# Channel order of the normalised activations, 2 KB pieces of the first expert table, and a buffer of its own for row gathers

## The chip, the cores and the metric

The kernel runs on one NeuronCore of one Trainium2 chip. The metric is the device time of one execution in microseconds (us); the median of 3 runs is what two kernels are compared by. TensorE (PE) multiplies, VectorE (DVE) and ScalarE (ACT) do elementwise work, GpSimd (POOL) issues the gathers by index here, SyncE (SP) and ACT issue the other transfers (DMA), which all share 16 DMA engines.

## The reference, cut to what matters

One layer of a decoder, for 256 prompt tokens and 32 sample tokens (288 columns in all), D = 2048 channels, float32: attention and convolution, the output projection `w_out`, then the expert layer PEER with 16384 experts, then a gate, then the final norm. PEER is the part that the change touches:

```
xc   = rmsnorm(h, ffn_norm)
qh   = xc @ peer_wq                        # product keys pick 8 x 16 experts a token
eidx, g = top-16 of the key sums, softmax
hpre = einsum('cd,ced->ce', xc, u[eidx])   # u, v: 16384 x 2048 each (128 MB each)
act  = gelu(hpre) * g
h   += einsum('ce,ced->cd', act, v[eidx])
```

## The kernel before

Activations lie transposed: `hT[p, dt, token]` holds channel on 128 partitions and 16 blocks `dt`. Every float32 product is made of three matmuls of a high and a low part (`tri`, lines 200 to 202), so each weight tile is split by ACT (`h`, line 186) and DVE (`l`, line 187) into two.

For the 256 prompt tokens the kernel does not gather: it multiplies by all 16384 experts in 128 tiles `t` of 128 experts. A **u tile** is loaded (`u_load`, `ur`, 1 MB in 8 DMAs of 32 partitions, four on SP and four on ACT), transposed in 32x32 blocks by DVE (`uT`, L923), split, and multiplied (`up`, 48 matmuls); GELU gives `ac`. The weights g are written out as a dense table in DRAM (`Gd`, `Gl`) by a one-hot stage and read back as `gt`. The **v loop** goes over 32 groups `g` of 4 tiles and 4 column blocks `u`, so 128 v steps: a 1 MB block of `peer_v` is loaded (`v`, L216, one DMA of 128 partitions on SP), split, multiplied by four `ac` tiles (`vps`, 48 matmuls in four PSUM banks) and added to `hT` by DVE (L490). 25 u tiles are made ahead, the other 103 inside the loop.

The 32 sample tokens do use gathers: 64 times POOL fetches 128 picked rows (1 MB, `fetch`, L1116): first 32 rows of `peer_u` (`ug`), each reduced with `xr` on DVE (L1135), then 32 rows of `peer_v` (`vg`), each added to `acc` on DVE (L1145). One `next(picked)` of `between` is one gather; the line of the loop says at which steps.

`raw_tile` gives the 1 MB buffers into which weights and gathered rows land: one ring of three (`WR`), handed out in program order to v blocks, `w_in`, `w_out`, `peer_wq` and `ple_gate` blocks, and to gathers alike. The order of instructions on each engine comes from a scheduler that simulates the program when it is built; engines take their own instructions strictly in that order, and so do the queues of SP, ACT and POOL.

Ahead of PEER, `w_out` streams (`wa0` to `wa3`) end in `residual`: DVE adds to `hT`, ACT squares (`sqh`, L485), DVE sums (`sq`). From the sum come `n2r` and the broadcast `rb2` (buffer `rb`); then `xf`, the normalised activations, is made block by block and `peer_wq` (`pq0` to `pq6`) is multiplied.

Of the kernel before, what the change touches and what calls it, by code (L numbers as in the profile page):

```python
# [10 lines left out]
F32 = mybir.dt.float32  # L11
# [124 lines left out]
def body(ctx: ExitStack, tc: tile.TileContext, A, O):  # L136
# [27 lines left out]

    conv_b, ln_g, ln_b = (cvec[:, 8 * i:8 * i + 8] for i in range(3))

    def raw_tile(name):
        return wp.tile([P, D], F32, tag="wr", name=name, bufs=WR)

    marks = {}  # L170

# [29 lines left out]
        nc.tensor.matmul(ps, ah, bl, start=False, stop=False)  # L201
        nc.tensor.matmul(ps, al, bh, start=False, stop=last)  # L202

    def load_block(src, b, cols, rows_by_lane, name, after=(), by_lane=False):
        n = sum(c[1] for c in cols)
        raw = raw_tile(name)
        v = raw[:, :4 * n].rearrange("p (j c) -> p j c", j=4)
        rows = src[512 * b:512 * b + 512]
        at = 0
        for c0, m in cols:  # L210
            if rows_by_lane:
                for a in range(4):
                    nc.sync.dma_start(v[32 * a:32 * a + 32, :, at:at + m],
                                      rows[128 * a:128 * a + 128, c0:c0 + m].rearrange("(j r) c -> r j c", j=4))
            else:
                nc.sync.dma_start(v[:, :, at:at + m], rows[:, c0:c0 + m].rearrange("(j p) c -> p j c", j=4))  # L216
            at += m
        with ExitStack() as order:
            for i in after:
                order.enter_context(tc.issue_after(i.ins))  # L220
            h, l = split(wp, raw[:, :4 * n], D, "w8", name, WB, by_lane)
        if by_lane:
            return lambda k, j, q=4 // cut[0]: [x[:, 512 * q * (k // q) + P * (q * j + k % q):][:, :P] for x in (h, l)]
        return lambda k, j, w=P: [x.rearrange("p (j c) -> p j c", j=4)[:, k, P * j:P * j + w] for x in (h, l)]
# [72 lines left out]
    def wide_pair(name):  # L297
        return [wide.tile([P, ND, T], F32R, tag="wide", name=f"{name}{k}") for k in "hl"]
# [494 lines left out]
    for k in range(CT):  # L793
        part(cat[:, k], xc[0][:, k], xc[1][:, k])
    sq2 = pa.tile([P, T], F32, tag="rb", name="sq2")
    for u in range(4):
        for j, ps in enumerate(stream(A["w_out"][0], [(512 * u, 512)], 4, xc, False, f"wa{u}", (0, 1), by_lane=True)):
            residual(pa, 4 * u + j, ps[:, :T], sq2, "sqh")
    ps_rb2 = spread(rstd_cols(pa, [sq2], D, "n2"), "ps_rb2")
    rb2 = keep.tile([P, T], F32, tag="rb2", name="rb2")  # L800
    marks["rb2"] = nc.vector.tensor_copy(rb2, ps_rb2[:, :T])
    pa_stack.close()

    cut[0] = 2
# [11 lines left out]
    pick = ab.tile([P, 3, TP], F32, tag="pick", name="pick")  # L816
    tk_stack = ExitStack()
    tk = tk_stack.enter_context(tc.tile_pool(name="tk", bufs=1, reuse_waits=RW))

    xf = wide_pair("xf")  # L820
    for dt in range(ND):
        f = tk.tile([P, T], F32, tag="nf", name=f"xf_{dt}", bufs=2)
        nc.vector.scalar_tensor_tensor(f, hT[:, dt], gain(1, dt), rb2, op0=ALU.mult, op1=ALU.mult)
        part(f, xf[0][:, dt], xf[1][:, dt])

    iob = tk.tile([P, 16, 16], BF16, tag="iob", name="iob")
    nc.gpsimd.tensor_copy(iob, iota[:, :16, None].to_broadcast([P, 16, 16]))
# [78 lines left out]
    def u_load(t):  # L906
        if t >= NE or t in urs:
            return
        ur = ff.tile([P, D], F32, tag="u8", name=f"ur{t}", bufs=UB)
        for k in range(2):  # L910
            rows = A["peer_u"][0, P * t + 64 * k:P * t + 64 * k + 64].rearrange("(c b) (u a x) -> a c b u x", c=32, a=4, x=P)
            for a in range(4):
                getattr(nc, UQ[a]).dma_start(
                    ur[32 * a:32 * a + 32, 1024 * k:1024 * k + 1024].rearrange("c (b u x) -> c b u x", b=2, u=4), rows[a])
        urs[t] = ur

    def u_steps(t):
        u_load(t)
        u_load(t + 1)
        ur = urs.pop(t)  # L920
        uT = ff.tile([P, D], F32, tag="u8", name=f"uT{t}", bufs=UB)
        for k in range(2):
            nc.vector.transpose(uT.rearrange("p (u j k c b) -> p k b u j c", u=4, j=4, k=2, c=32)[:, k],  # L923
                                ur.rearrange("p (k b u j r) -> p k b u j r", k=2, b=2, u=4, j=4)[:, k])
        hr, lr = split(ff, uT, D, "u8", f"u{t}", UB)
        mm = None
        for u in range(5):
            if u > 0:
                mm = mm or mm_ps(f"up{t}")
                for dt in range(4 * u - 4, 4 * u):  # L930
                    s = slice(P * dt, P * dt + P)
                    tri(mm[:, :TP], (hr[:, s], lr[:, s]), (xf[0][:, dt, :TP], xf[1][:, dt, :TP]), dt == 0, dt == ND - 1)
            if u < 4:
                yield
        ac = ff.tile([P, T], F32, tag="ac", name=f"ac{t}", bufs=AB)[:, :TP]
        nc.scalar.activation(ac, mm[:, :TP], AF.Gelu)  # L936
        if t < LS:
            nc.sync.dma_start(Ad[t], ac)
        else:
            acts[t] = ac  # L940
        yield
# [13 lines left out]
    PQA = [marks[k] for k in PQK]  # L955
    for h in range(NH):
        if h % 2 == 0:
            qps = stream(A["peer_wq"][0], [(256 * h, 512)], 4, xf, True, f"pq{h}",
                         after=lambda b: PQA if h == 0 and b >= PQN else ())
        skT = sub_keys(h)  # L960
        qh = tk.tile([P, 2, T], F32, tag="qh", name=f"qh{h}", bufs=1)
        for n in range(2):
            nc.scalar.copy(qh[:, n], qps[2 * (h % 2) + n][:, :T])
        if h % 4 == 0:
            pss = ax_ps(f"pss{h}")
        for n in range(2):
            nc.tensor.matmul(pss[32 * (h % 4):32 * (h % 4) + 32, P * n:P * n + P], qh[:, n, TP:T], skT[:, n],
                             start=True, stop=True, tile_position=(0, 32 * (h % 4)))
        psp = ax_ps(f"psp{h}")
        for i in range(2):  # L970
            for n in range(2):
                c0 = 256 * i + 128 * n
                nc.tensor.matmul(psp[:, c0:c0 + P], qh[:, n, 128 * i:128 * i + 128], skT[:, n], start=True, stop=True)
        for i in range(2):
            for n in range(2):
                c0 = 256 * i + 128 * n
                sixteen(val[:, 2 * h + i, n], ind[:, 2 * h + i, n], psp[:, c0:c0 + P], P, f"wk{h}{i}{n}")
        if h >= 6:
# [76 lines left out]
    def v_part(g, between):  # L1055
# [11 lines left out]
            nc.vector.tensor_mul(v, v, gts[t // GK][:, :, t % GK])  # L1067
            hl.append(split(gpool, acts[t], TP, "ah", f"a{t}", AHB))
        for u in range(4):
            at = load_block(A["peer_v"][0], g, [(512 * u, 512)], False, f"v{g}_{u}", by_lane=True)  # L1070
            for j in range(4):
                ps = ax_ps(f"vps{g}_{u}{j}")
                for k in range(GRP):
                    tri(ps[:, :TP], at(k, j), hl[k], k == 0, k == GRP - 1)
                residual(None, 4 * u + j, ps[:, :TP], None, "")
            between(u)
            if last:
                gated_norm(range(4 * u, 4 * u + 4))
# [33 lines left out]
                nc.vector.tensor_add(sq3, sq3, q)  # L1112

    def fetch(src, s, name):
        gb = raw_tile(name)
        nc.gpsimd.indirect_dma_start(out=gb, out_offset=None, in_=src,  # L1116
                                     in_offset=bass.IndirectOffsetOnAxis(ap=eix[:, s // 16, s % 16:s % 16 + 1], axis=0))
        return gb

    def picked_steps():  # L1120
        xs = raw_tile("xs")
        c = slice(TP, T)
        x4 = [x[:, :, c].bitcast(F32)[:, :, None, :].to_broadcast([P, ND, 4, TS]) for x in xf]
        nc.vector.tensor_tensor(out=xs.rearrange("p (d a t) -> p d a t", d=ND, a=4), in0=x4[0], in1=x4[1], op=ALU.add)
# [1 line left out]
        for u in range(4):  # L1126
            ps = ax_ps(f"xsp{u}")
            for j in range(4):
                dt = 4 * u + j
                nc.tensor.transpose(ps[:, P * j:P * j + P], xs[:, P * dt:P * dt + P], ident)  # L1130
            nc.scalar.copy(lanes(xr[:, 512 * u:512 * u + 512]), turn(ps))
        gb = fetch(A["peer_u"][0], 0, "ug0")
        yield
        for s in range(32):
# [7 lines left out]
        for s in range(32):  # L1142
# [27 lines left out]
    for g in range(NE // GRP):  # L1170
        reload(g + 1)
        if g == NE // GRP - SIDE:
            gB = side_inputs()
        if g == NE // GRP - 1:
            xg = wide_pair("xg")
            sq3 = ff.tile([P, T], F32, tag="ac", name="sq3", bufs=AB)
        v_part(g, lambda u: (u_next(GRP * g + GRP + LK), next(picked, None) if g < 4 or u % 2 else None))
    gp_stack.close()
    pc_stack = ExitStack()
    pc = pc_stack.enter_context(tc.tile_pool(name="pc", bufs=1, reuse_waits=RW))  # L1180
# [78 lines left out]
```

## Time and profile before

| what | value |
|---|---|
| median of 3 runs (lowest, highest) | 2391.47 us (2390.91, 2402.99) |
| the profiled execution | 2391.9 us |
| its span, first to last instruction | 2389.9 us |
| granted TensorE clock, mean | 0.975 of full |
| PE, DVE, ACT busy | 94%, 81%, 42% of the span |
| bytes moved by DMA | 479.29 MB, 201 GB/s |

In the rows below, an "x" is a count of instructions, and a wait is idle time of an engine put down to what ended it. Numbers of windows are microseconds from the start of the span.

### The profile page before, as it was taken

How to read it: one execution, taken by the hardware profiler on the slowest of the kernel's cores; microseconds unless marked ns; L12 is line 12 of the kernel's file. 1: busy time of each engine (PE TensorE's matmuls, PEld its weight loads, DVE VectorE, ACT ScalarE, POOL GpSimd, SP SyncE). 2: the span in 40 equal slices, each digit the busy share in tenths (PEclk: the TensorE clock that was granted, in tenths of full speed). 3: DMA queues.
4: the chain of work that ended last, by engine and by line, in shares of the span. 5: the costliest groups of instructions: out<-in, count | busy, mean ns of one | idle time of the engine just before them, and what ended most of it. 6: DMA issues, size and time to landing. Idle time of an engine off the chain costs nothing.

```text
span 2389.9 us, 44695 instructions
## 1 busy us (share of the span) xinstructions
PE 2250.0 (94%) x17715; PEld 2205.2 (92%) x17715; DVE 1933.2 (81%) x3343; ACT 1007.0 (42%) x1623; POOL 165.2 (7%) x168
## 2 busy tenths in 40 slices
PE   6999999889889898999999999999999999999997
PEld 5999989889789888999999999999999999999997
DVE  5999844699989788989888787878888887877854
ACT  3453344343478533344333333333434343334533
POOL 2033140000000011100000000000000000000000
PEclk9999999999989998999999999999999999999998
DMA  7757442784558999999788798888989888975663
GB/s 197 172 125 172 107 142 89 168 170 87 132 146 217 260 282 279 300 260 269 245 233 238 212 241 224 222 237 219 243 222 241 213 230 221 237 211 172 169 134 83
DMA packets 474175, 479.29 MB, mean 201 GB/s; under 512 B 35785, under 2 KB 361825, under 8 KB 465374
## 3 DMA queue, kind: packets, MB, share of 16 engines
q1 hardware_dynamic: 306894, 309.03, 49.6%
q10 hardware_dynamic: 154672, 93.74, 16.5%
q0 software_dynamic: 12400, 73.66, 9.4%
q8 instruction: 139, 2.28, 0.4%
q14 instruction: 70, 0.57, 0.1%
HBM read 454.17 MB, written 23.00 MB: 200 GB/s over the span
## 4 chain that ended last, share of the span: by engine, by line
PE 49%; DMA 24%; DVE 13%; issue 10%; ACT 2%; SPq 1%; ACTq 0%; POOL 0%; DVEq 0%; POOLq 0%
DMA ur<-in_peer_u 7%; DMA vg<-in_peer_v,eix 7%; DMA v<-in_peer_v 5%; PE vps L200 4%; PE vps L202 4%; PE vps L201 4%; PE up L201 3%; PE up L202 3%; PE up L200 3%; DVE uT L923 3%; DMA gt<-Gd 1%; DVE v_0l L187 1%; DMA Gd<-stg 1%; DVE hT L490 1%; DMA gt<-Gl 1%
## 5 line engine op out<-in xcount | busy, mean ns | idle before, releaser
L923 DVE STREAM_TRANSPOSE uT<-ur 128x1024 f32<-128x1024 f32 x256 | 304.0, 1221 | 24.5 <-PE up L201 11.1
L490 DVE TENSOR_TENSOR hT<-hT,vps 128x256 f32<-128x256 f32 x512 | 199.4, 410 | 20.4 <-PE vps L202 20.2
L936 ACT ACTIVATE ac<-up 128x256 f32<-128x256 f32 x128 | 49.3, 387 | 369.1 <-DVE hT L490 114.7
L1145 DVE SCALAR_TENSOR_TENSOR acc<-vg,hot,acc 128x2048 f32<-128x2048 f32 x31 | 72.9, 2352 | 120.0 <-DMA vg<-in_peer_v,eix 120.0
L1135 DVE CUSTOM_DVE_ANT_0 ug<-ug,xr 128x2048 f32<-128x2048 f32 x32 | 73.1, 2286 | 29.0 <-DMA ug<-in_peer_u,eix 28.9
L1116 POOL DMA_INDIRECT ug<-in_peer_u,eix x32 | 39.6, 1238 | 749.6 <-DVE uT L923 324.6
L186 ACT CAST v_0h<-v 128x1024 fp32r<-128x1024 f32 x64 | 63.8, 1044 | 58.5 <-PE vps L201 32.0
L186 ACT CAST v_3h<-v 128x1024 fp32r<-128x1024 f32 x64 | 63.8, 1046 | 42.6 <-PE vps L201 20.7
L1116 POOL DMA_INDIRECT vg<-in_peer_v,eix x32 | 30.0, 937 | 746.4 <-DVE v_3l L187 367.8
L187 DVE TENSOR_TENSOR v_0l<-v,v_0h 128x1024 fp32r<-128x1024 f32 x64 | 75.7, 1216 | 6.1 <-ACT v_0h L186 6.1
L186 ACT CAST v_2h<-v 128x1024 fp32r<-128x1024 f32 x64 | 63.8, 1045 | 39.5 <-PE vps L201 24.0
L187 DVE TENSOR_TENSOR v_1l<-v,v_1h 128x1024 fp32r<-128x1024 f32 x64 | 75.7, 1215 | 2.4 <-ACT v_1h L186 2.4
L1041 PE MATMUL gp<-at,bt 128*128 128x128 f32 x512 | 68.0, 280 | 9.5 <-ACT at L1034 6.0
L187 DVE TENSOR_TENSOR v_2l<-v,v_2h 128x1024 fp32r<-128x1024 f32 x64 | 75.7, 1215 | 1.1 <-ACT v_2h L186 1.1
L187 DVE TENSOR_TENSOR v_3l<-v,v_3h 128x1024 fp32r<-128x1024 f32 x64 | 75.7, 1212 | 0.9 <-ACT v_3h L186 0.9
L1041 PEld LDWEIGHTS gp<-at,bt 128*128 128x128 f32 x512 | 62.9, 194 | 11.7 <-ACT at L1034 7.4
L186 ACT CAST v_1h<-v 128x1024 fp32r<-128x1024 f32 x64 | 64.0, 1046 | 19.1 <-DMA v<-in_peer_v 12.6
L1034 ACT ACTIVATE at<-eqa,pick 128x128 f32<-128x128 bf16 x192 | 64.3, 428 | 4.2 <-DVE eqa L1031 2.7
L457 DVE SCALAR_TENSOR_TENSOR cat<-cat,cw 128x256 f32<-128x256 f32 x120 | 52.7, 479 | 0.0
L1067 DVE TENSOR_TENSOR ac<-ac,gt 128x256 f32<-128x256 f32 x112 | 43.4, 391 | 8.0 <-DMA gt<-Gl 4.9
L1044 ACT COPY stg<-gp 128x256 f32<-128x256 f32 x128 | 41.8, 395 | 16.7 <-PE gp L1041 6.2
L1038 DVE TENSOR_TENSOR bt<-iota,pick 128x512 f32<-128x512 f32 x64 | 43.2, 679 | 0.0
(5771 smaller groups left out, 9874.7 us busy)
## 6 DMA issues: line engine op xcount, KB each, us to landing
v<-in_peer_v SPq DMA_DIRECT2D x128, 1024.0 KB
ur<-in_peer_u SPq DMA_DIRECT2D x512, 128.0 KB
ur<-in_peer_u ACTq DMA_DIRECT2D x512, 128.0 KB
Gd<-stg SPq DMA_DIRECT2D x14, 1024.0 KB
gt<-Gd ACTq DMA_DIRECT2D x32, 448.0 KB
gl0b<-in_w_in SPq DMA_DIRECT2D x32, 128.0 KB
gl1b<-in_w_in SPq DMA_DIRECT2D x32, 128.0 KB
gl2b<-in_w_in SPq DMA_DIRECT2D x32, 128.0 KB
```

What stands on the lines that cost most here:

```text
L186: marks["part"] = nc.scalar.copy(y, x)
L187: marks["sub"] = nc.vector.tensor_sub(z, x, y.bitcast(F32))
L200: nc.tensor.matmul(ps, ah, bh, start=first, stop=False)
L201: nc.tensor.matmul(ps, ah, bl, start=False, stop=False)
L202: nc.tensor.matmul(ps, al, bh, start=False, stop=last)
L490: nc.vector.tensor_add(x, x, ps)
L923: nc.vector.transpose(uT.rearrange("p (u j k c b) -> p k b u j c", u=4, j=4, k=2, c=32)[:, k], ur.rearrange("p (k b u j r) -> p k b u j r" ...
L1034: nc.scalar.activation(at[:, k], eq[:, :, k], AF.Copy, scale=pick[:, 2, t0 + k:t0 + k + 1])
L1041: nc.tensor.matmul(ps[:, P * k:P * k + P], bt[:, k], at[:, k], start=True, stop=True)
L1116: nc.gpsimd.indirect_dma_start(out=gb, out_offset=None, in_=src, in_offset=bass.IndirectOffsetOnAxis(ap=eix[:, s // 16, s % 16:s % 16 + 1] ...
L1135: nc.vector.tensor_tensor_reduce(out=gb, in0=gb, in1=xr, scale=1.0, scalar=0.0, op0=ALU.mult, op1=ALU.add, accum_out=hot[:, s // 16, s % 1 ...
L1145: nc.vector.scalar_tensor_tensor(acc, gb, w, acc, op0=ALU.mult, op1=ALU.add)
```

## The change

Four edits. First, `xf` gets another order of channels. Before, partition p of block dt is channel 128 dt + p, up to a swap of 32-wide parts inside each 512. Now partitions 32a to 32a + 31 of `xf` hold channels 512a to 512a + 511. `hT` keeps its order; while `w_out` ends, ACT copies 32 partitions at a time from `hT`, times the norm's gain, into a new tile `hg` (64 activations), and `xf` is made from `hg` times `rb2` by 16 DVE multiplications in place of 16 that took `hT`, gain and `rb2` at once. Second, u tiles and `peer_wq` are loaded to fit: a row's part for one set of 32 partitions is then one piece of 2 KB, where it was four pieces of 512 B. The number of DMAs, bytes, transposes and matmuls is the same. Third, the ring of three is cut into three named slots: v blocks take slots 0 and 1 in turn, gathers slot 2 alone, all others still go round the three. Fourth, gathers are called at 9 of 16 steps throughout, where it was each step of the first 16 and then every other.

```diff
-    def raw_tile(name):
-        return wp.tile([P, D], F32, tag="wr", name=name, bufs=WR)
+    turns = [0]
+
+    def raw_tile(name, slot=None):
+        if slot is None:
+            slot = turns[0] % WR
+            turns[0] += 1
+        return wp.tile([P, D], F32, tag=f"wr{slot}", name=name, bufs=1)
...
+    hg = pa.tile([P, ND, T], F32, tag="cat", name="hg")
     for u in range(4):
         for j, ps in enumerate(stream(A["w_out"][0], [(512 * u, 512)], 4, xc, False, f"wa{u}", (0, 1), by_lane=True)):
-            residual(pa, 4 * u + j, ps[:, :T], sq2, "sqh")
+            dt = 4 * u + j
+            residual(pa, dt, ps[:, :T], sq2, "sqh")
+            for a in range(4):
+                s = slice(32 * a, 32 * a + 32)
+                nc.scalar.activation(hg[32 * u:32 * u + 32, 4 * a + j], hT[s, dt], AF.Copy, scale=gain(1, dt)[s])
...
+    xf = wide_pair("xf")
+    for dt in range(ND):
+        nc.vector.tensor_mul(hg[:, dt], hg[:, dt], rb2)
+        part(hg[:, dt], xf[0][:, dt], xf[1][:, dt])
     pa_stack.close()
...
-    xf = wide_pair("xf")
-    for dt in range(ND):
-        f = tk.tile([P, T], F32, tag="nf", name=f"xf_{dt}", bufs=2)
-        nc.vector.scalar_tensor_tensor(f, hT[:, dt], gain(1, dt), rb2, op0=ALU.mult, op1=ALU.mult)
-        part(f, xf[0][:, dt], xf[1][:, dt])
...
-            rows = A["peer_u"][0, P * t + 64 * k:P * t + 64 * k + 64].rearrange("(c b) (u a x) -> a c b u x", c=32, a=4, x=P)
+            rows = A["peer_u"][0, P * t + 64 * k:P * t + 64 * k + 64].rearrange("(c b) (a x) -> a c b x", c=32, a=4)
             for a in range(4):
                 getattr(nc, UQ[a]).dma_start(
-                    ur[32 * a:32 * a + 32, 1024 * k:1024 * k + 1024].rearrange("c (b u x) -> c b u x", b=2, u=4), rows[a])
+                    ur[32 * a:32 * a + 32, 1024 * k:1024 * k + 1024].rearrange("c (b x) -> c b x", b=2), rows[a])
...
-            at = load_block(A["peer_v"][0], g, [(512 * u, 512)], False, f"v{g}_{u}", by_lane=True)
+            at = load_block(A["peer_v"][0], g, [(512 * u, 512)], False, f"v{g}_{u}", by_lane=True, slot=u % 2)
...
     def fetch(src, s, name):
-        gb = raw_tile(name)
+        gb = raw_tile(name, 2)
...
-        v_part(g, lambda u: (u_next(GRP * g + GRP + LK), next(picked, None) if g < 4 or u % 2 else None))
+        v_part(g, lambda u: (u_next(GRP * g + GRP + LK), next(picked, None) if (4 * g + u) * 9 // 16 != (4 * g + u - 1) * 9 // 16 else None))
```

What the scheduler makes of it. On DVE in the middle of the v loop, before, one addition of a gathered row (`acc`) stands among two v steps; these eleven rows, of one u tile, hold the one of gather 7.

```order
L187 TENSOR_TENSOR v15_1l_16923<-v15_1_16920,v15_1h_16922 128x1024 x2
L187 TENSOR_TENSOR a65l_17335<-ac65_16490,a65h_17334 128x256
L923 STREAM_TRANSPOSE uT69_16993<-ur69_16851 128x2x16x32 x2
L1067 TENSOR_TENSOR ac67_16759<-ac67_16759,gt16_17325 128x256
L490 TENSOR_TENSOR hT_79<-hT_79,vps15_00_16795 128x256
L187 TENSOR_TENSOR a66l_17340<-ac66_16626,a66h_17339 128x256
L490 TENSOR_TENSOR hT_79<-hT_79,vps15_01_16809 128x256
L187 TENSOR_TENSOR u69l_16997<-uT69_16993,u69h_16996 128x1024
L490 TENSOR_TENSOR hT_79<-hT_79,vps15_02_16823 128x256
L1145 SCALAR_TENSOR_TENSOR acc_15638<-vg7_17323,hot_4858,acc_15638 128x2048
L187 TENSOR_TENSOR u69l_16997<-uT69_16993,u69h_16996 128x1024
```

After, on DVE at nearly the same place, two such additions, of gathers 10 and 11, stand one u tile apart.

```order
L1155 SCALAR_TENSOR_TENSOR acc_16797<-vg10_19046,hot_4973,acc_16797 128x2048
L192 TENSOR_TENSOR v13_3l_16104<-v13_3_16101,v13_3h_16103 128x1024
L932 STREAM_TRANSPOSE uT66_16602<-ur66_16457 128x2x16x32 x2
L192 TENSOR_TENSOR v13_3l_16104<-v13_3_16101,v13_3h_16103 128x1024
L1076 TENSOR_TENSOR ac64_16388<-ac64_16388,gt16_17362 128x256
L496 TENSOR_TENSOR hT_79<-hT_79,vps13_20_15973 128x256
L496 TENSOR_TENSOR hT_79<-hT_79,vps13_21_15987 128x256
L496 TENSOR_TENSOR hT_79<-hT_79,vps13_22_16001 128x256
L496 TENSOR_TENSOR hT_79<-hT_79,vps13_23_16015 128x256
L192 TENSOR_TENSOR v14_0l_16260<-v14_0_16257,v14_0h_16259 128x1024 x2
L192 TENSOR_TENSOR u66l_16606<-uT66_16602,u66h_16605 128x1024
L1155 SCALAR_TENSOR_TENSOR acc_16797<-vg11_19338,hot_4973,acc_16797 128x2048
```

Counted over the whole order on DVE: before, the 64 gathers are taken up one a step in v steps 0 to 15 and then every second step, the last at v step 108; now the first is at v step 1 and the last at v step 78, 1.22 steps apart on the mean (the calls stand at 9 of 16 steps, and the scheduler pulls them forward).

On DVE between `rb` (the broadcast norm) and the work on `peer_wq`, before, each block of `xf` is multiplied and split in turn.

```order
L801 COPY rb_4848<-ps_rb_4844 128x288
L808 TENSOR_REDUCE sel<-ident 128x32
L187 TENSOR_TENSOR pq0b1l<-pq0b_5008,pq0b1h 128x1024 x2
L823 SCALAR_TENSOR_TENSOR xf_4870<-hT,vecs,rb_4848 128x288
L823 SCALAR_TENSOR_TENSOR xf_4874<-hT,vecs,rb_4848 128x288
L187 TENSOR_TENSOR xfl<-xf_4870,xfh 128x288
L823 SCALAR_TENSOR_TENSOR xf_4878<-hT,vecs,rb_4848 128x288
L187 TENSOR_TENSOR xfl<-xf_4874,xfh 128x288
```

After, at the same place, 15 multiplications stand ahead of the first low part `xfl`.

```order
L812 COPY rb_4913<-ps_rb_4909 128x288
L192 TENSOR_TENSOR pq0b1l<-pq0b_5057,pq0b1h 128x1024 x2
L815 TENSOR_TENSOR hg<-hg,rb_4913 128x288 x15
L192 TENSOR_TENSOR xfl<-hg,xfh 128x288 x15
L815 TENSOR_TENSOR hg<-hg,rb_4913 128x288
L192 TENSOR_TENSOR xfl<-hg,xfh 128x288
```

The transposes and u splits that stood between the blocks of `xf` now stand behind them.

On ACT at the end of the last `w_out` stream, after, four copies into `hg` stand behind each square.

```order
L491 ACTIVATE sqh_4878<-hT 128x288
L809 ACTIVATE hg<-hT,vecs 32x288 x4
L491 ACTIVATE sqh_4886<-hT 128x288
L809 ACTIVATE hg<-hT,vecs 32x288 x4
L250 ACT_TABLE_LOAD
L250 ACTIVATE n2r<-n2v 128x3
```

Before, the same rows are the squares alone, one behind the other, and then the table load and `n2r`.

## Rows read from the trace of the kernel before

**Rows 1.** The page's busy time of each engine.
```profile
PE 2250.0 (94%) x17715; PEld 2205.2 (92%) x17715; DVE 1933.2 (81%) x3343; ACT 1007.0 (42%) x1623; POOL 165.2 (7%) x168
```
**Rows 2.** Windows by stage, busy time of each engine, clock, DMA share.
```profile
core 0: us, PE busy (x) PEld busy (x) DVE busy (x) ACT busy (x) POOL busy (x), PEclk, DMA share, GB/s
460.00:510.00 50.00, 36.75 (x235) 34.22 (x235) 37.38 (x64) 23.63 (x39) 0.51 (x1) 0.86 0.99 192
600.00:800.00 200.00, 173.94 (x1421) 169.56 (x1421) 189.74 (x441) 137.83 (x370) 0.00 (x0) 0.96 0.67 178
800.00:1010.00 210.00, 184.28 (x1428) 181.80 (x1428) 175.53 (x234) 78.27 (x117) 23.89 (x16) 0.92 0.99 281
1010.00:1200.00 190.00, 190.00 (x1592) 190.00 (x1591) 170.57 (x240) 79.66 (x104) 11.24 (x12) 1.00 0.90 262
1200.00:2140.00 940.00, 906.24 (x7464) 899.97 (x7464) 776.83 (x979) 357.18 (x466) 34.46 (x36) 0.99 0.86 228
```
**Rows 3.** Waits of PE from 1200 to 2100 us, all there are.
```profile
engine line waited for: us in total, times, longest us
PE vps L200 <- DVE hT L490: 33.7, 30, 2.9
```
**Rows 4.** Waits of DVE from 1200 to 2100 us, the longest.
```profile
DVE acc L1145 <- DMA vg<-in_peer_v,eix: 120.0, 31, 4.9
```
**Rows 5.** Timeline of POOL, first and last fetch, and one.
```profile
1311.86 0.94 POOL L1116 DMA_INDIRECT vg<-in_peer_v,eix  x1 [22.06 <-DVE v_3l L187]
...
1894.37 0.94 POOL L1116 DMA_INDIRECT vg<-in_peer_v,eix  x1 [23.55 <-DVE v_3l L187]
...
2065.19 0.94 POOL L1116 DMA_INDIRECT vg<-in_peer_v,eix  x1 [23.47 <-DVE v_1l L187]
```
**Rows 6.** Timeline of DVE, where that fetch is used.
```profile
1902.78 2.35 DVE L1145 SCALAR_TENSOR_TENSOR acc<-vg,hot,acc 128x2048 f32<-128x2048 f32 x1 [3.72 <-DMA vg<-in_peer_v,eix]
```
**Rows 7.** Waits of POOL from 1200 to 2100 us, the longest.
```profile
POOL vg L1116 <- DVE v_3l L187: 367.8, 16, 24.2
```
**Rows 8.** Waits of SP's queue from 1200 to 2100 us, the longest.
```profile
SPq L216 <- DMA vg<-in_peer_v,eix: 281.0, 32, 10.3
```
**Rows 9.** Waits of ACT from 800 to 1010 us, the longest.
```profile
ACT v_3h L186 <- DMA v<-in_peer_v: 16.8, 3, 6.2
ACT v_2h L186 <- DMA v<-in_peer_v: 15.4, 4, 5.1
```
**Rows 10.** Waits of DVE for gathers from 1010 to 1200 us.
```profile
DVE ug L1135 <- DMA ug<-in_peer_u,eix: 7.1, 5, 3.0
```
**Rows 11.** DMA from 1200 to 2100 us: queue, packets, MB, share.
```profile
q1 hardware_dynamic: 119998, 116.62, 48.5%
q10 hardware_dynamic: 86513, 49.04, 24.0%
```
**Rows 12.** DMA from 2250 to 2350 us, where only `ple_gate` loads.
```profile
DMA packets 7876, 14.44 MB, mean 144 GB/s; under 512 B 880, under 2 KB 880, under 8 KB 7867
...
q1 hardware_dynamic: 7867, 14.31, 66.2%
```
**Rows 13.** Timeline of ACT, end of the `w_out` streams.
```profile
411.98 1.44 ACT L186 CAST cath<-cat 128x288 fp32r<-128x288 f32 x4
...
434.40 1.91 ACT L186 CAST wa2b1h<-wa2b 128x2048 fp32r<-128x2048 f32 x1 [0.52 <-PE wa1a L201]
...
460.60 0.44 ACT L485 ACTIVATE sqh<-hT 128x288 f32<-128x288 f32 x1 [1.15 <-DVE hT L490]
...
462.69 0.20 ACT L244 ACTIVATE n2r<-n2v 128x3 f32<-128x3 f32 x1 [0.35 <-DVE n2v L261]
```
**Rows 14.** Timeline of DVE, the norm and the first `xfl`.
```profile
436.34 2.29 DVE L187 TENSOR_TENSOR wa2b1l<-wa2b,wa2b1h 128x2048 fp32r<-128x2048 f32 x1 [1.03 <-ACT wa2b1h L186]
...
464.98 0.46 DVE L801 COPY rb<-ps_rb 128x288 f32<-128x288 f32 x1 [1.08 <-PE ps_rb L267]
...
468.90 0.46 DVE L187 TENSOR_TENSOR xfl<-xf,xfh 128x288 fp32r<-128x288 f32 x1
```

More of the change, by code (lines that the diff above doesn't have):

```diff
@@ L202, in tri, with load_block @@
         nc.tensor.matmul(ps, al, bh, start=False, stop=last)
-    def load_block(src, b, cols, rows_by_lane, name, after=(), by_lane=False):
+    def load_block(src, b, cols, rows_by_lane, name, after=(), by_lane=False, slot=None):
         n = sum(c[1] for c in cols)
-        raw = raw_tile(name)
+        raw = raw_tile(name, slot)
         v = raw[:, :4 * n].rearrange("p (j c) -> p j c", j=4)
@@ L212, in load_block @@
                 for a in range(4):
+                    r0 = 512 * b + 128 * a if rows_by_lane == 1 else 512 * a + 128 * b
                     nc.sync.dma_start(v[32 * a:32 * a + 32, :, at:at + m],
-                                      rows[128 * a:128 * a + 128, c0:c0 + m].rearrange("(j r) c -> r j c", j=4))
+                                      src[r0:r0 + 128, c0:c0 + m].rearrange("(j r) c -> r j c", j=4))
             else:
@@ L922, in u_steps @@
         for k in range(2):
-            nc.vector.transpose(uT.rearrange("p (u j k c b) -> p k b u j c", u=4, j=4, k=2, c=32)[:, k],
-                                ur.rearrange("p (k b u j r) -> p k b u j r", k=2, b=2, u=4, j=4)[:, k])
+            nc.vector.transpose(uT.rearrange("p (d k c b) -> p k b d c", d=ND, k=2, c=32)[:, k],
+                                ur.rearrange("p (k b d r) -> p k b d r", k=2, b=2, d=ND)[:, k])
         hr, lr = split(ff, uT, D, "u8", f"u{t}", UB)
@@ L957, in body @@
         if h % 2 == 0:
-            qps = stream(A["peer_wq"][0], [(256 * h, 512)], 4, xf, True, f"pq{h}",
+            qps = stream(A["peer_wq"][0], [(256 * h, 512)], 4, xf, 2, f"pq{h}",
                          after=lambda b: PQA if h == 0 and b >= PQN else ())
@@ L1120, in picked_steps @@
     def picked_steps():
-        xs = raw_tile("xs")
+        xs = raw_tile("xs", 2)
         c = slice(TP, T)
@@ L1130, in picked_steps @@
                 nc.tensor.transpose(ps[:, P * j:P * j + P], xs[:, P * dt:P * dt + P], ident)
-            nc.scalar.copy(lanes(xr[:, 512 * u:512 * u + 512]), turn(ps))
+            nc.scalar.copy(xr.rearrange("p (a d r) -> p d a r", a=4, d=ND)[:, 4 * u:4 * u + 4],
+                           ps.rearrange("p (j a r) -> p j a r", j=4, a=4))
         gb = fetch(A["peer_u"][0], 0, "ug0")
@@ L1150, in picked_steps @@
                 yield
-        at = raw_tile("accp")
+        at = raw_tile("accp", 2)
         nc.vector.tensor_copy(turn(at), lanes(acc))
```

## The prediction

> **What bounds the kernel now.** The page's first part says that PE is busy 94% of the span and DVE 81% [rows 1], but a busy PE need not be a full one, so I went on to windows by stage. Each matmul of the v loop costs a fixed time where nothing disturbs it: from 1010 to 1200 us PE is busy all the time and makes 1592 matmuls, so 190 / 1592 = 119.3 ns each [rows 2]. A step of the loop with a u tile has 48 + 48 matmuls, 11.46 us. From 1200 to 2140 us there are 7464 matmuls in 940 us [rows 2]; at 119.3 ns they need 890.7 us. So 49.3 us of this stretch are not matmul work (a few records may be missing, so this is an upper bound), 0.63 us for each of its 77.75 steps. From 800 to 1010 us the same sum gives 1428 x 119.3 = 170.4 us, so 39.6 us of 210 are lost, at a DMA share of 0.99 and a granted clock of 0.92 [rows 2]. From 600 to 800 us DVE is busy 189.74 of 200 us [rows 2]: that stage is DVE's and the change takes nothing from DVE there.
>
> The table of waits says what the 49.3 us are. PE waits for one thing only: for the addition to `hT`, which frees its PSUM bank, 33.7 us in 30 waits [rows 3]. DVE is late with it because it stands still for a gathered row 31 times, 120.0 us [rows 4]. One turn: POOL starts a fetch at 1894.37, behind 23.55 us of waiting for a v block's split (`v_3l`), the row is used at 1902.78 after DVE has idled 3.72 us [rows 5, 6]. So 8.4 us from fetch to use, and the fetch starts late not because the earlier row is in use, but because its buffer in the shared ring still holds a v block (367.8 us of such waits [rows 7]). The other way round, v loads wait for gathered rows in that ring, 281.0 us on SP's queue [rows 8], but there ACT seldom notices; it does from 800 to 1010 us, where it waits for v blocks, 16.8 and 15.4 us in the two largest rows [rows 9]. Of the loop's fetches by `vg`, 32 stand between 1311.86 and 2065.19 us [rows 5], 24.3 us apart: two steps of 12.15 us, not 11.46.
>
> **The change, part by part.**
>
> *Own buffer for gathers.* A fetch now waits only for the row before it to be used. A turn is then 2.35 us of addition [rows 6] and 8.4 us to the next use, 10.8 us. The new order takes the 64 gathers up 1.22 steps apart, 1.22 x 11.46 = 14.0 us, so each row should lie ready 3 us early, and the stall of rows 4 goes. Does DVE then have room, with 0.82 gathers a step up to v step 78? From 1010 to 1200 us there are 1592 / 96 = 16.6 steps and 12 fetches, 0.72 a step, DVE is busy 170.57 us, 10.3 us a step, waits 7.1 us for rows, and PE loses nothing [rows 2, 10]. A further 0.10 gathers of about 2.4 us make 10.5 us a step, 92% of 11.46. So it fits, with 0.96 us to spare. From v step 79 on there are none at all. What is late next is PE itself. The gain lies between the 33.7 us of named waits [rows 3] and 49.3 us [rows 2]; I take 40.
>
> *2 KB pieces.* In the loop ACT's queue carries little but u pieces: 86513 packets in 24.0% of 16 x 900 us, 39.9 ns each [rows 11], so 160 ns for 2 KB, and 2048 packets / 16 engines x 39.9 ns = 5.1 us of all engines for a tile. What does a 2 KB piece to 32 partitions cost beside other traffic? The trace has no such row, so two bounds. SP's queue has 119998 packets and 116.62 MB; if they are 512 B and 2 KB, 35.9 thousand are v's 2 KB, and with 39.9 ns for the small ones, (0.485 x 14400 us - 84.1 thousand x 39.9 ns) / 35.9 thousand = 101 ns [rows 11]. But v is written to 128 partitions at once. `ple_gate` is 2 KB to 32 partitions from one queue: 66.2% of 1600 us for 7867 - 880 = 6987 pieces, 152 ns [rows 12]. A tile would cost 512 / 16 x 101 = 3.2 us, or 4.9 us. The u tile is like the gate in its 32 partitions and like v in that two queues feed different partitions at once; I take 125 ns, 4.0 us, a fall of 1.1 us a tile.
>
> The trace shows the 32-partition loads at 152 ns where the 128-partition ones take 101 [rows 11, 12]. The Trainium skill, page "SBUF — State Buffer", section "Door 1: The DMA port swizzle", would have it so: 32 partitions reach half of the ports, 189 GB/s against 328 at 1 MiB, and two transfers to different partitions gain only 6%. By its figure a tile of 1.05 MB takes 5.5 us in any pieces, no less than the 5.1 us now, and the sum would be the first rival's.
>
> Where does this land? In the steady loop the share is 0.86 and PE does not wait for DMA [rows 2, 3], so nothing there; it pays where the share is 0.99, from 800 to 1010 us. There the order also puts 12 gathers in the first 16 v steps where it was 16: 4 fewer at about 3 us of all engines (a gathered MB at the v rate, 512 x 101 / 16 = 3.2 us), 13 us, and some 13 u tiles (u24 to u36 in the order) at 1.1 us, 14 us. That is 27 of 208 us of DMA time, against 39.6 us lost. Bounds 0 and 39.6; since PE there also restarts at a lower clock and v's two buffers leave a load no run-ahead, I take 20.
>
> *v blocks in two slots.* In the loop a slot is free again when its block is split, about a step before it is multiplied, and is wanted two steps later: 20 us for a load, where a gather takes 8.4 with its issue. Hidden by PE's 11.46 us a step; nothing. In the last v steps without u tiles a step is half as long; up to 0.5 us for each of 10, inside the rounding of the 40.
>
> *`hg` and the norm.* 64 copies on ACT; four like instructions take 1.44 us [rows 13], so 0.36 each, 23 us of ACT. In three of the four streams the cast of the next block stands behind three squares and now 12 copies, 4.3 us. That cast starts at 434.40 and its low part ends at 436.34 + 2.29 = 438.63 [rows 13, 14]; PE is through with the stream before at about 434.4, when the cast's buffer comes free, and wants the block half a stream later (48 matmuls of 288 columns, 48 x 119.3 x 288 / 256 ns = 6.4 us), at 440.8: 2.2 us of cover, 2.1 us late, 3 times, 6 us. At the end the last square waits for the copies of the blocks before and `n2r` for four more, about 3 us on the path from 460.60 to 462.69 [rows 13]. Then 15 multiplications of about 0.45 us stand ahead of the first `xfl`, which came 3.9 us behind `rb` [rows 14]: 15 x 0.45 - 1 = 5.8 us. PE is the one that waits, and the clock falls with it. Against this, once begun, the new order starves PE less: from 460 to 510 us PE is now busy only 36.75 of 50 us at a clock of 0.86 [rows 2], with DVE doing u tiles between the blocks of `xf`. Bounds: 3 us (all but the ACT tail is won back) and 18 (6 + 3 + 5.8, and 3 for a slower clock). I take 8 lost.
>
> Transposes have the same shape before and after in the order, so no change. Sum, against the profiled execution of 2391.9 us, which is within 0.5 us of the median 2391.5: 2391.9 - 40 - 20 + 8 = 2339.9, **2340 us**.
>
> **The rivals.**
>
> *Pieces to 32 partitions are no cheaper* (152 ns or more [rows 12]). Then 800 to 1010 us gains from fewer gathers only, 8 us, and up to v step 78 the DMA engines get 3.2 + 5.1 + 0.82 x 3.2 = 10.9 us of work and some for `gt` in each 11.46 us step, so rows land late and only the 39 steps without gathers gain, 39 x 0.63 = 25. 2391.9 - 25 - 8 + 8 = 2367. For it: rows 12; against it: two queues. Chance 0.24.
>
> *DVE becomes the bound up to v step 78.* At 92% on the mean, bunched gathers or bursts of splits let `hT` be late and PE waits on. I give back half of the 40: 2360. For it: rows 2 show DVE at 90% from 1010 us; against it: PE is full there. Chance 0.14.
>
> *Nothing moves*: what PE gains in the loop is spent ahead of PEER (18 us and more) and v loads in two slots are late, 2385 to 2395. Chance 0.08.
>
> *Slower: the single gather buffer.* There is no second row in flight, so fetch to use enters each turn. It decides where a turn is longer than 14.0 us by more than DVE's spare 1.17 us (1.22 x 0.96) and 52 us / 64 = 0.8 us, that is 14.0 + 2.0 - 2.35 = 13.6 us from fetch to use, against 8.4 now [rows 5, 6]. At 14.5 us: 64 x (14.5 + 2.35 - 14.0 - 1.17) = 108 us, 2448 us. Chance 0.07.
>
> **How the numbers follow.** My forecast has 0.47. 0.5% is 12 us, about what a measurement here can tell from no change. Forecast and the first two rivals are all under 2380, so faster 0.85; same 0.08, slower 0.07. The forecast's own range, from the distances of its three terms to their bounds added as squares, is 2318 to 2363. For 8 in 10 the range must hold the first two rivals as well and so reaches up to 2382; downward, all terms at their better end give 2391.9 - 49.3 - 39.6 + 3 = 2306, of which I take 2312.
>
> **What would show it.** Right: the wait of DVE for `vg` nearly gone, PE without waits for `hT` behind 1200 us, the loop's steps at 11.5 us, a DMA share near 0.9 at 800 to 1010 us, `ur` in 2 KB packets near 125 ns, and PE idle some 6 us longer behind the last `w_out` stream. Wrong: DVE waits for gathers each 14 us, u packets at 150 ns or more, or PE waiting for v splits whose loads came late.

## The result, and the profile after

| | us |
|---|---|
| changed kernel, median of 4 runs (lowest, highest) | 2351.3 (2347.1, 2359.4) |
| kernel before, beside it, 4 runs | 2391.2 (2389.8, 2403.0) |
| ratio, 95% interval | 0.9826 (0.9802 to 0.9849) |
| profiled execution; its span; granted clock | 2350.5; 2348.8; 0.976 |

The change saves about 40 us; 52 were forecast, and the range held it. Windows of the changed kernel over the stretches of [rows 2] (x is a count, then clock and DMA share):

```profile
460.00:510.00 50.00, 31.86 (x197) 30.31 (x197) 31.59 (x61) 30.57 (x53) 0.00 (x0) 0.76 0.53 119
600.00:800.00 200.00, 175.72 (x1417) 171.52 (x1417) 189.34 (x509) 127.57 (x331) 0.63 (x1) 0.95 0.55 155
800.00:1010.00 210.00, 193.34 (x1560) 190.92 (x1560) 181.88 (x258) 94.31 (x165) 13.52 (x11) 0.96 0.91 275
1010.00:1200.00 190.00, 190.00 (x1592) 189.95 (x1591) 178.36 (x234) 76.71 (x102) 16.08 (x14) 1.00 0.87 274
1200.00:2140.00 940.00, 937.23 (x7824) 936.00 (x7823) 818.89 (x1038) 380.09 (x490) 51.20 (x39) 1.00 0.79 238
```

The last line says that the loop now loses 940 - 7824 x 0.1193 = 6.6 us where it lost 49.3. From 800 to 1010 us it loses 23.9 where it lost 39.6. The first line says the opposite: ahead of PEER PE is busy 31.86 us of 50, 5 less than before, at a lower clock, and DMA is half idle.

Waits of PE, DVE (1200 to 2100 us) and POOL (800 to 2100 us) in the changed kernel, one line of each; they answer to [rows 3, 4, 7].

```profile
PE vps L205 <- DVE hT L496: 1.7, 1, 1.7
DVE acc L1155 <- DMA vg<-in_peer_v,eix: 10.1, 6, 3.1
POOL vg L1125 <- DVE acc L1155: 328.4, 29, 16.4
```

A fetch now waits for the row before it and no longer for a v block's split (one of 32 fetches of `vg` excepted, 11.8 us), and DVE's idle time for rows fell from 120.0 to 10.1 us.

Timeline of ACT, then of DVE, in the changed kernel around the end of the `w_out` streams [rows 13, 14]:

```profile
457.56 2.17 ACT L809 ACTIVATE hg<-hT,vecs 32x288 f32<-32x288 f32 x4
459.75 1.90 ACT L191 CAST wa3b1h<-wa3b 128x2048 fp32r<-128x2048 f32 x1
...
475.40 0.44 ACT L491 ACTIVATE sqh<-hT 128x288 f32<-128x288 f32 x1
475.87 2.20 ACT L809 ACTIVATE hg<-hT,vecs 32x288 f32<-32x288 f32 x4
478.08 1.28 ACT L250 ACT_TABLE_LOAD   x1
479.38 0.20 ACT L250 ACTIVATE n2r<-n2v 128x3 f32<-128x3 f32 x1
```
```profile
481.67 0.46 DVE L812 COPY rb<-ps_rb 128x288 f32<-128x288 f32 x1 [1.09 <-PE ps_rb L273]
482.04 2.35 DVE L192 TENSOR_TENSOR pq0b1l<-pq0b,pq0b1h 128x1024 fp32r<-128x1024 f32 x2
484.31 5.61 DVE L815 TENSOR_TENSOR hg<-hg,rb 128x288 f32<-128x288 f32 x15
489.84 2.29 DVE L192 TENSOR_TENSOR xfl<-hg,xfh 128x288 fp32r<-128x288 f32 x6
```

Four copies take 2.17 us, and they stand in the way of the next cast and square. The last square comes at 475.40 (460.60 before), the first `xfl` at 489.84 (468.90).

To compare kernels, three places cut each span: the last addition of `wb3a` (ahead of every edit), the last copy `stg` out of `gp` (end of the one-hot stage), and the last addition of the v loop. Each is the last start in a tile's view; of the changed kernel:

```profile
L496 DVE TENSOR_TENSOR hT<-hT,wb3a x4: 448/453/454, 401.9 to 408.4; 128x288 f32<-128x288 f32 x4
L1053 ACT COPY stg<-gp x128: 358/385/486, 693.1 to 832.4; 128x256 f32<-128x256 f32 x128
L496 DVE TENSOR_TENSOR hT<-hT,vps x512: 370/411/423, 871.1 to 2213.3; 128x256 f32<-128x256 f32 x171
```

So 424.0 us from the first to the second and 1380.9 to the third. "Early loss" is 200 us less the matmuls at 119.3 ns, from 10 us ahead of the end of `gp` on, with the fetches there; for the kernel before, the stretch of [rows 2].

| kernel | median us | ratio (95%) | to `wb3a` | to `gp` | to loop end | early loss (fetches) |
|---|---|---|---|---|---|---|
| before | 2391.2 | | 408.1 | 407.6 | 1439.2 | 39.6 (16) |
| changed | 2351.3 | 0.9826 (0.9802, 0.9849) | 408.4 | 424.0 | 1380.9 | 24.0 (12) |
| buf_cad | 2351.6 | 0.9791 (0.9723, 0.9858) | 416.1 | 406.9 | 1388.0 | 31.2 (11) |
| buf_only | 2350.3 | 0.9786 (0.9718, 0.9855) | 417.7 | 407.3 | 1388.9 | 30.4 (11) |
| cad_only | 2383.4 | 0.9924 (0.9893, 0.9955) | 416.3 | 405.8 | 1416.9 | 27.7 (12) |
| pieces_only | 2389.3 | 0.9954 (0.9923, 0.9985) | 416.6 | 426.2 | 1424.5 | 44.2 (16) |
| after_again | 2352.1 | 0.9828 (0.9796, 0.9860) | 408.6 | 425.3 | 1389.0 | 33.3 (11) |
| hg_pool | 2376.8 | 0.9928 (0.9904, 0.9952) | 406.9 | 440.3 | 1392.3 | |
| mul_order | 2363.8 | 0.9881 (0.9849, 0.9913) | 408.9 | 431.3 | 1384.1 | |
| hg_free | 2349.0 | 0.9812 (0.9781, 0.9844) | 408.0 | 416.6 | 1387.6 | |
| hg_q4 | 2356.8 | 0.9831 (0.9806, 0.9855) | 407.0 | 423.8 | 1388.7 | |
| hg_off | 2347.7 | 0.9800 (0.9776, 0.9824) | 406.6 | 410.5 | 1394.4 | 34.4 (12) |
| hg_off_late | 2327.0 | 0.9713 (0.9689, 0.9737) | 408.3 | 411.4 | 1372.6 | 18.2 (5) |
| buf_only_again | 2337.0 | 0.9752 (0.9726, 0.9778) | 407.3 | 406.6 | 1389.2 | 31.1 (11) |

Behind the loop all take 135 us more. The parts come from the one execution that was profiled, which can lie off the median: pieces_only's took 2404.0 us, 14.7 above it, cad_only's 2375.8, 7.6 below, and after_again's 2360.0, 7.9 above. The experiments ran in three groups of four, in the order of the table, each beside runs of the kernel before (2398.5, 2393.8 and 2395.2 us). The part up to `wb3a`, which no edit touches, took 7 to 11 us longer in the first group than in the others, so medians are compared within a group, by ratio, or by the later parts.

### The profile page after: what moved, and what is told of

Read it like the earlier page. It is cut to its first block, busy times and chain, and to the rows that moved or that the text cites. A ratio compares the mean times of both kernels' runs of the same rounds, so it can differ in the third digit from the quotient of the medians.

```text
span 2348.8 us, 44821 instructions
## 1 busy us (share of the span) xinstructions
PE 2238.2 (95%) x17715; PEld 2198.7 (94%) x17715; DVE 1937.3 (82%) x3343; ACT 1043.8 (44%) x1687; POOL 176.3 (8%) x168
## 4 chain that ended last, share of the span: by engine, by line
PE 80%; DMA 9%; DVE 6%; ACT 3%; issue 1%; SPq 1%; ACTq 0%; DVEq 0%
PE vps L205 9%; PE vps L207 9%; PE vps L206 9%; PE up L206 8%; PE up L205 8%; PE up L207 8%; DMA ur<-in_peer_u 4%; DMA v<-in_peer_v 2%; DVE uT L932 1%; DMA Gd<-stg 1%; ACT hg L809 1%; PE gp L1050 1%; ACT at L1043 1%; ACT stg L1053 0%; PE pso L716 0%
## 5 line engine op out<-in xcount | busy, mean ns | idle before, releaser
L1155 DVE SCALAR_TENSOR_TENSOR acc<-vg,hot,acc 128x2048 f32<-128x2048 f32 x31 | 72.6, 2341 | 10.1 <-DMA vg<-in_peer_v,eix 10.1
L1050 PEld LDWEIGHTS gp<-at,bt 128*128 128x128 f32 x512 | 62.5, 193 | 10.5 <-ACT at L1043 7.4
L1125 POOL DMA_INDIRECT vg<-in_peer_v,eix x32 | 43.2, 1349 | 358.2 <-DVE acc L1155 328.4
```

What stands on the lines that cost most here:

```text
L1050: nc.tensor.matmul(ps[:, P * k:P * k + P], bt[:, k], at[:, k], start=True, stop=True)
L1155: nc.vector.scalar_tensor_tensor(acc, gb, w, acc, op0=ALU.mult, op1=ALU.add)
```

## The experiments

**Which edit carries the gain.** Theory: the own buffer; rivals: the new order, or the 2 KB pieces. Four kernels took the edits apart; the diffs are parts of the change's own.

```diff
 buf_only, against before (buf_cad: this and the line of cad_only)
+        return wp.tile([P, D], F32, tag=f"wr{slot}", name=name, bufs=1)
+            at = load_block(..., by_lane=True, slot=u % 2)
+        gb = raw_tile(name, 2)
 cad_only, against before
+... next(picked, None) if (4 * g + u) * 9 // 16 != (4 * g + u - 1) * 9 // 16 else None
 pieces_only, against the changed kernel
+        return wp.tile([P, D], F32, tag="wr", name=name, bufs=WR)
+... next(picked, None) if g < 4 or u % 2 else None
```

> The kernel before with two slots for the v blocks, a buffer of its own for gathers and the new order of the gathers; no hg, u and the norm as before (512 B pieces). Theory (the own buffer removes the stall of the loop; the pieces pay only from 800 to 1010 us; hg costs about 17 us ahead of PEER): loop minus 40, nothing for hg, some 10 us less from 800 to 1010 us through fewer gathers, so 2341 us, 2335 to 2356. DVE's wait for vg under 20 us, PE's for hT under 5 us between 1200 and 2100 us. Rival (the rows come on time only because u needs fewer DMA packets): DVE still waits over 60 us for vg, and the time is 2365 us or more.

> The kernel before with the slots and the gather buffer alone; gathers in the old order, one a step in the first 16 v steps, then every second. Theory: the stall of the loop goes in the old order too (a row has 22.9 us and needs 8.4), so minus 40 from 1200 us on; from 800 to 1010 us as before or some us worse, since one row a step of 11.5 us leaves no slack with one buffer: 2355 us, 2348 to 2370. Rival (the new order does it): 2380 us or more.

> The kernel before with the new order of the gathers alone; one shared ring of three buffers. Theory: fetches still wait for a v block's split, DVE still idles about 3.7 us for nearly each row, so the loop loses as much as before or more up to the last gather and nothing behind it: 2380 us, 2365 to 2400, DVE's wait for vg over 60 us. Rival (the new order does it): 2355 us or less.

> The changed kernel with the shared ring of three buffers and the old order of the gathers: hg, the order of 512 channels and the 2 KB pieces stay. Theory: the stall of the loop stays (DVE waits about 100 us for vg, PE about 30 us for hT), hg costs 17 us, the pieces give back some 8 us from 800 to 1010 us: 2400 us, 2388 to 2408. Rival (the pieces carry the gain): 2375 us or less.

DVE's waits for v rows from 1200 to 2100 us in buf_only, cad_only and pieces_only:

```profile
DVE acc L1150 <- DMA vg<-in_peer_v,eix: 8.1, 6, 2.9
```
```profile
DVE acc L1145 <- DMA vg<-in_peer_v,eix: 96.6, 28, 5.6
```
```profile
DVE acc L1150 <- DMA vg<-in_peer_v,eix: 109.3, 31, 5.6
```

The buffer alone takes 120.0 us of waiting to 8.1 and makes the kernel at least as fast as the whole change; the new order on top of it adds nothing (1388.0 us of loop against 1388.9). The other two leave the stall in place and have 0.5 to 0.8%. buf_cad came 10 us above its forecast, 8 of them in the opening that no edit touches; the other three lie in their ranges with that opening (buf_only and pieces_only would lie below without it).

pieces_only shows one thing that its forecast did not have. PE's wait for `hT` from 1200 to 2100 us, and the window from 1200 to 2140 us:

```profile
PE vps L200 <- DVE hT L491: 17.3, 23, 1.9
```
```profile
1200.00:2140.00 940.00, 922.63 (x7668) 917.17 (x7668) 800.36 (x1014) 369.21 (x482) 36.42 (x38) 1.00 0.79 234
```

PE waits half as long as before (33.7 us), and 940 - 7668 x 0.1193 = 25.2 us are lost in place of 49.3, though DVE still waits 109.3 us. So with the shared ring the rest of the change does save time in the loop, in this one profile; why, no run shows.

**What `hg` costs.** The changed kernel takes 16.4 us more to `gp` than the one before, the kernel before with the buffer none. Theory: its 64 copies on ACT, then also the order of the multiplications, then the memory it lies in.

```diff
 hg_pool
+                nc.gpsimd.tensor_scalar(hg[32 * u:32 * u + 32, 4 * a + j], hT[s, dt], gain(1, dt)[s], None, op0=ALU.mult)
 mul_order
+        f = pa.tile([P, T], F32, tag="n4", name=f"xf_{dt}", bufs=2)
+        nc.vector.tensor_mul(f, hg[:, dt], rb2)
+        part(f, xf[0][:, dt], xf[1][:, dt])
 hg_free: as mul_order, with the gain (hgain) in the multiplication, and
+    def lane_copy(op, u, a):
+        op(hg[32 * u:32 * u + 32, 4 * a:4 * a + 4], hT[32 * a:32 * a + 32, 4 * u:4 * u + 4])
+            if u:
+                lane_copy(nc.gpsimd.tensor_copy, u - 1, j)
+    for a in range(4):
+        lane_copy(nc.scalar.copy if a % 2 else nc.gpsimd.tensor_copy, 3, a)
```

> The changed kernel itself, beside the three versions below: 2351 us, 2343 to 2360 on every theory. Its opening up to the end of the last stream before hg (407 to 418 us in the profiles so far) shows what differs from run to run without a change.

> The changed kernel with the 64 copies into hg on POOL, which has nothing else there. Theory (the copies on ACT cost some 11 us, since they stand ahead of casts and squares): the last square comes 8 to 11 us earlier than in the changed kernel, and the time is 2342 us, 2336 to 2349; if POOL takes over 0.8 us for a copy its tail gives back up to 8 us. Rival (the 15 multiplications ahead of the first low part are the cost): 2351 us, 2346 to 2358.

> The changed kernel with the product by rb in a tile of its own with two buffers, so that two multiplications stand ahead of the first low part in place of 15. Theory (the order of the multiplications costs 4 to 6 us of the 17): first low part 5 us behind rb in place of 8, the first stream of PEER begins 4 to 6 us earlier, 2346 us, 2340 to 2353. Rival (PE starts with the high parts anyway and waits for weights): 2351 us, 2346 to 2358.

> The changed kernel with hg made off the path: 16 plain copies of 32 x 1152, 14 of them on POOL during the next stream and 2 on ACT behind the last square, the gain in the multiplication by rb, and that in two buffers. Theory (hg costs 16 to 19 us, all of it for its place on ACT and for the order): the span from the end of the last stream before hg to the first low part falls from 81 us to 62 to 66, and the time is 2335 us, 2328 to 2344, faster than the changed kernel by 0.5% and more. Rival (the opening's loss comes from DMA: w_out and wq blocks land late): 2348 us or more.

The copies by tile in hg_pool (min/median/max ns, first and last start), and the wait of PE that follows from them:

```profile
L809 POOL TENSOR_SCALAR hg<-hT,vecs x64: 993/1003/3072, 416.6 to 506.0; 32x288 f32<-32x288 f32 x64
```
```profile
PE pq0a L205 <- ACT xfh L191: 30.4, 4, 22.8
```

The same in hg_free:

```profile
L809 POOL COPY hg<-hT x14: 1138/1276/3286, 422.2 to 461.7; 32x1152 f32<-32x1152 f32 x14
L809 ACT COPY hg<-hT x2: 1147/1148/1148, 461.0 to 462.1; 32x1152 f32<-32x1152 f32 x2
```

hg_pool was 25 us slower than the changed kernel in place of 9 faster: a copy takes 1.00 us on POOL (0.53 on ACT), the last one starts 47 us behind the last square (at 459.4, as early as before), and PE waits 30.4 us. ACT is freed, as the theory said, but POOL becomes the bound. hg_free has a quarter of the copies. Its first low part comes 62.5 us behind `wb3a`, as forecast, and its first PEER stream begins 15 us earlier than in the changed kernel; at `gp` 7 to 9 us of that are left, and the median is 3 us lower in place of 16, at the time of its rival though the low part came as the theory said. mul_order fell: its first low part came 4 us earlier and it was 12 us slower. Timeline of SP's queue in mul_order, in the changed kernel and in the kernel before, the loads of u0, and the wait of that queue in the changed kernel (470 to 510 us):

```profile
484.71 20.76 SPq L219 DMA_DIRECT2D pq2b<-in_peer_wq  x12
509.55 3.58 SPq L923 DMA_DIRECT2D ur<-in_peer_u  x3
```
```profile
484.42 1.74 SPq L219 DMA_DIRECT2D pq2b<-in_peer_wq  x4
496.98 3.53 SPq L922 DMA_DIRECT2D ur<-in_peer_u  x5
```
```profile
459.27 4.77 SPq L913 DMA_DIRECT2D ur<-in_peer_u  x4
468.00 1.74 SPq L213 DMA_DIRECT2D pq2b<-in_peer_wq  x4
```
```profile
SPq L922 <- DVE xfl L192: 10.7, 1, 10.7
```

u0's load stands behind three `pq2b` blocks in place of one, u0 and u1 are split 20 and 16 us later (530 and 542 us), and DVE, which is busy 95% of 600 to 800 us, ends later. Before, that load goes out ahead of all `pq2b`, 38 us earlier than in the changed kernel; there it waits for the last `xfl` (10.7 us). That `hg` lies over the memory of the first u buffer was the next theory.

```diff
 hg_q4: hg in four tiles of another tag
+    hq = [pa.tile([P, 4, T], F32, tag="q4", name=f"hg{a}", bufs=4) for a in range(4)]
 hg_off: the copies of hg_free into hq, f in a ring of four, and in u_steps
+        if t < 1:
+            with tc.high_priority(offset=4000):
+                u_load(0)
+                u_load(1)
 hg_off_late: hg_off and
+... next(picked, None) if 4 * g + u >= 16 and (4 * g + u) % 8 < 5 else None
```

> The changed kernel with hg in four other buffers of the same pool, which do not lie over the memory of the first u tiles; copies on ACT and 15 multiplications ahead of the first low part as in the changed kernel. Theory (hg holds the memory of the first u tile's buffer up to the last low part of xf, so its load comes at 497 us in place of 459, and the stage bound by DVE ends later): u0's load starts by 486 us, u0 and u1 are split some 10 us earlier, and the one-hot stage (gp) ends 5 to 9 us earlier than in the changed kernel; 2344 us, 2338 to 2350. Rival (only the copies on ACT and the order of the multiplications cost time): gp ends within 2 us of the changed kernel, 2351 us.

> All three costs of hg off the path: plain copies of 32 x 1152 on POOL and ACT as in the version before, other buffers, four multiplications ahead of the first low part, and the loads of u0 and u1 with a higher priority. Theory (these three are the whole cost of hg): gp ends 407 to 410 us behind the end of the last w_out stream before hg, as in the kernel before, where the changed kernel takes 424; 2338 us, 2331 to 2346. Rival (what PE gains at the start of PEER is given back in the stage that DVE bounds, as in the version before, where gp took 416.6 us): 2348 us or more.

> The same, with the first gather at v step 16 or later and then five in eight steps, so that the first 200 us behind gp hold none. Theory (gathers take DMA time where the loop starts): the 200 us from 10 us ahead of gp's end lose 15 us in place of the 24 to 33 that all versions with an own gather buffer lose, and the time is 8 to 15 us under the version without the late gathers. Rival (PE's restart at the lower clock and the u and v tiles themselves are the loss): within 4 us of that version.

> The kernel before with the slots and the gather buffer alone, once more, beside the three versions above on one chip. Theory (2 KB pieces are worth 0 to 5 us, hg costs 16): this edit alone is as fast as the changed kernel or up to 10 us faster, ratio 0.978 to 0.982, and 3 to 12 us slower than the version with all of hg off the path. Rival (pieces worth 10 us and more): over 12 us slower than that version.

Loads of u0 in hg_q4 on SP's queue and on ACT's, and its first transpose on DVE:

```profile
485.15 12.46 SPq L923 DMA_DIRECT2D ur<-in_peer_u  x5
```
```profile
497.56 0.67 ACTq L923 DMA_DIRECT2D ur<-in_peer_u  x1
```
```profile
502.00 1.25 DVE L933 STREAM_TRANSPOSE uT<-ur 128x1024 f32<-128x1024 f32 x1 [1.43 <-DMA ur<-in_peer_u]
```

SP's half of the load begins 12 us earlier, but ACT's half only at 497.56, behind the loads of the sub-keys (498.81 in the changed kernel), so the transpose gains 2 us and `gp` 0 to 2: this theory fell, the memory alone is not the cost. With copies, order, memory and the loads' place mended together (hg_off), `gp` ends 410.5 us behind `wb3a`, 13.5 of the 16.4 us back. hg_off's time was still 10 us above the forecast: its loop takes 1394.4 us. Why it does is not settled.

Windows of 200 us around the loop's start in pieces_only, hg_off and hg_off_late:

```profile
832.80:1032.80 200.00, 170.48 (x1306) 167.01 (x1304) 162.31 (x217) 68.13 (x95) 23.79 (x16) 0.92 0.91 275
```
```profile
807.10:1007.10 200.00, 176.62 (x1388) 174.13 (x1387) 161.79 (x220) 73.29 (x100) 14.22 (x12) 0.93 0.86 266
```
```profile
809.70:1009.70 200.00, 187.90 (x1524) 185.68 (x1523) 158.58 (x239) 83.17 (x113) 4.76 (x5) 0.97 0.81 249
```

They lose 44.2, 34.4 and 18.2 us with 16, 12 and 5 fetches (hg_off_late was to have none there), and hg_off_late is 20.7 us faster than hg_off, more than forecast. It beats both kernels: 2327.0 us, ratio 0.9713 (0.9689 to 0.9737). But buf_only_again, 2337.0, is 10.7 us faster than hg_off, so my forecast of its place fell: the buffer alone beats the change with nearly all of `hg`'s cost removed. It stands at 0.9752 (0.9726 to 0.9778) where the whole change stood at 0.9826 and 0.9828, each beside its own runs of the kernel before: the other three edits together take back some 0.7% (about 18 us), near what `hg` costs up to `gp`. buf_only, with a wider interval, does not tell.

## Why the prediction came out as it did

*Own buffer, 40 us: right.* The stall of [rows 4] went, the loop gave 42.7 us (49.3 less 6.6) between the bounds of 33.7 and 49.3, and buf_only shows that the buffer alone does it. PE is next, as written, and DVE fits: it is busy 178.36 of 190 us from 1010 us on, and PE loses nothing there. The rival with DVE as the bound and the slower one with a single buffer are out.

*2 KB pieces and fewer early gathers, 20 us: 15.7 in one profile and 6.3 in another, and not through the pieces.* The price was right. From 1250 to 1290 us ACT's queue carries almost only u pieces in the changed kernel:

```profile
q10 hardware_dynamic: 1062, 1.64, 15.6%
```

At most 1.64 MB / 2048 B = 800 are pieces; 0.156 x 640 us less 0 to 39.9 ns for each of the other 262 makes 112 to 125 ns a piece, where I took 125, so 3.6 to 4.0 us a tile, against 152 ns a piece in the first rival. The Trainium skill, page "SBUF — State Buffer", section "Door 1: The DMA port swizzle", gives 189 GB/s to 32 partitions, by estimate 5.5 us a tile; the measurement decides against it here.

What failed is the step "Where does this land?". It put the pieces at nothing in the loop, and at 14 of 27 us of DMA time in the early stretch. With the gathers' own buffer the cheaper pieces lower the DMA share (0.85 to 0.79 from 1200 to 2140 us between buf_only and the changed kernel) and give no time that can be told from the spread: buf_cad, with the old pieces and the same calls, loses 31.2 us early, the changed kernel 24.0 and 33.3 in its two profiles, with loops of 1388.0, 1380.9 and 1389.0 us. pieces_only loses 44.2 us early, no less than the 39.6 of before, though in the loop, with the shared ring, it loses 25.2 in place of 49.3. The early loss goes with the number of gathers instead. Windows of cad_only, then of the changed kernel in its two profiles:

```profile
812.10:1012.10 200.00, 180.38 (x1444) 176.95 (x1443) 166.51 (x235) 77.77 (x107) 13.29 (x12) 0.97 0.94 276
```
```profile
822.40:1022.40 200.00, 183.57 (x1475) 181.44 (x1474) 170.77 (x229) 76.78 (x105) 15.20 (x12) 0.96 0.91 280
```
```profile
823.90:1023.90 200.00, 177.65 (x1397) 174.80 (x1397) 163.31 (x221) 73.48 (x101) 13.52 (x11) 0.93 0.87 265
```

Two pairs differ in the calls of the gathers alone: before and cad_only, (39.6 - 27.7) / 4 = 3.0 us a gather, and hg_off and hg_off_late, (34.4 - 18.2) / 7 = 2.3. The step had 3 us of DMA time for each of four, the other half of its term. By estimate from these two prices, 9 to 12 us come from the four gathers fewer.

*`hg` and the norm, 8 us: the term that was mis-sized.* It cost 16.4 to 17.7 us in two profiles, at the bound of 18. A copy over 32 partitions takes 0.53 us, not the 0.36 taken from a 128-partition cast [rows 13]: 34 us of ACT, not 23, so the last square is 14.8 us late where 6 + 3 were worked out. The Trainium skill, page "ScalarE: Activation LUTs", section "What ACT_TABLE_LOAD costs", would have sized it: 186 ns and 0.833 ns a column, 93 ns more for a scale read from a tile, measured there on 128 partitions; by estimate 426 ns for a square and 519 ns for a copy with its gain. The trace agrees, on 32 partitions too: 444 and 532 ns. The 15 multiplications added 6.1 us to the first `xfl` (20.9 less 14.8), as the 5.8 said. What should have given time back did not: I counted on PE starving less once begun, but the first u tiles, done by DVE between the blocks of `xf` before, now come behind them (u0 at 510 us, 485 before), and the stage behind is DVE's.

*The rival "nothing moves"* had the right price for the opening (18 us), and failed in the loop.

Sum: -42.7 - 15.7 + 16.4 = -42.0 against -52. Profile against profile it is 2391.9 - 2350.5 = 41.4. The term of the early stretch is the loose one: after_again's profile, 2360.0 us, has 6.3 there and not 15.7.

Still open: why the loop of pieces_only lost less; whether the pieces are worth anything once `hg` is free, since hg_off and buf_only differ in the order of many instructions; and late gathers with the buffer alone, which was not run.

## What to carry to other kernels

Look first for two kinds of loads in one ring of buffers: when the slow one waits for a buffer that the fast one holds, one slot of its own can be worth more than cheaper transfers, as it was here. A layout that makes a load cheaper pays only where DMA ends the wait, and its rearranging must be priced as the instructions that it becomes, with their own shapes, and with the buffers that they keep from what comes next. After such a change, see which transfers can leave the stretch that is still bound: here calling the first gathers 16 steps later, which brought the first fetch 97 us later (960.8 us against 864.0 in hg_off), gave half as much as the change itself.

## What was not expected of the hardware

A copy of 32 x 288 with a scale takes 0.53 us on ACT, and a square of 128 x 288 beside it 0.44: fewer partitions do not make it cheaper. One of 32 x 1152 takes 1.15 us on ACT and 1.28 on POOL, but 32 x 288 with a scale takes 1.00 on POOL: a quarter of the elements for three quarters of the time, though the two operations differ.
